# A deeper ring of expert weights, paid for with single buffers, in a mixture-of-experts decoder block

## The chip, the cores and the metric

One core of one Trainium2 chip runs the whole program. The engines are TensorE (PE: matmuls, and PEld: the weight loads that go with them), VectorE (DVE), ScalarE (ACT), GpSimd (POOL) and SyncE (SP). DMAs are issued from the queues of SP, ACT and POOL and carried out by 16 DMA engines that all of them share. The metric is the device time of one execution in microseconds (us), the median of several runs; less is better.

## The reference

The block normalises its input, runs a convolution branch and a differential attention branch, merges the two through gates and an output projection, and then sends each of the 1024 tokens (1024 wide) to 2 of 32 experts. Only the last part is touched by the change:

```python
def expert_block(args):
    toks, wb, e = args
    xb = hf[toks]                                   # 128 gathered rows
    hid = jax.nn.silu(jnp.matmul(xb, w_g[e])) * jnp.matmul(xb, w_u[e])
    return jnp.matmul(hid, w_d[e]) * wb[:, None]
...
y = jnp.zeros_like(hf).at[row_tok].add(yb.reshape(n_rows, D))
```

`w_g` and `w_u` are 1024 x 512 and `w_d` is 512 x 1024 in each of the 32 experts, all float32: 6 MiB of weights for each expert, 192 MiB in all, each used once.

## The kernel before

The program runs through the projections, the attention and the convolution branch, the merge, the output projection with the routing (`out_proj`), and then the experts, one after the other (`experts`).

**Weights.** The weights of an expert arrive in six chunks of 1 MiB (128 partitions x 2048 numbers): two of the gate matrix G, two of the up matrix U, two of the down matrix D. SP issues the loads (`chunk_dma`). A chunk lands in one of the 12 slots of a ring: 11 in the pool mrA, one in mrB, which lies where the merged activations `mg` lay before. The load that takes a slot again waits until the chunk that lay there has been split. From the 18th load on, a load also waits until the load five before it has landed, so at most five are under way.

**Splits.** Matmuls run on pairs of numbers in a shortened float format, a high and a low part, three matmuls for each product (`mm3`, lines 98 to 100). For each chunk ACT writes the high part `ch` (line 93) and DVE the low part `cl` (line 94). Both have four buffers (`nsplit`): the fifth chunk waits until PE is done with the first.

**One expert.** POOL gathers the 128 rows of the expert's tokens from HBM into `gx` (line 1003, an indirect DMA; two buffers, `ngx`). PE transposes them in two halves of four blocks into `pt` (line 1015), ACT and DVE split the result into `xh` and `xl` (two buffers each). PE multiplies by G (24 matmuls) and U (24), ACT and DVE form the hidden tile `sg`, PE transposes it (line 1044), ACT and DVE split it into `dh` and `dl`, PE multiplies by D (24), ACT scales the result into `y` (line 1057, two buffers, `ny`), and POOL adds it to the output in HBM (line 1058, an indirect DMA that adds).

**Order of the work.** Experts overlap: `experts` writes down, for each expert e, the load of expert e+1, a gather, the matmuls by G of e, the transposes of the hidden tile of e-1, the matmuls by U of e, the transposes of the rows of e+1, and the matmuls by D of e-1. A scheduler with its own idea of durations then sets the order on each engine; the order is fixed when the program is built, and each engine works through its list without overtaking. Where the scheduler expects the weights late, it moves the transposes of the next rows forward: in the kernel before, from the rows of expert 23 on, the first of them stand ahead of matmuls by G or U of the expert before, not behind its matmuls by U.

The lines that the change and the prediction speak of: `out_proj` with `mg_split`, which reads `mg` last; `chunk_dma`, `chunk_split`, `gather`, `x_front`, `expert_down` and `experts`; and in `block_kernel` the pools from `mg` to `moe`.

Of the kernel before, what the change touches and what calls it, by code (L numbers as in the profile page):

```python
# [10 lines left out]
F32 = mybir.dt.float32  # L11
F32R = mybir.dt.float32r
# [8 lines left out]
P = 128  # L21
D = 1024
T = 1024
NT = T // P
ND = D // P
# [5 lines left out]
E = 32  # L31
# [18 lines left out]
class Block:  # L50
    def __init__(self, tc, ins, outs, dbg=None):
        self.tc, self.nc = tc, tc.nc
        self.i = ins
        self.out = outs[0]
        self.dbg = dbg or {}
        self.groups = {2: (0, 2), 4: (2, 2), 6: (4, 2), 7: (6, 1)}
        self.modeB, self.modeC = 99, 31
        self.loads, self.window, self.rawA, self.rawB, self.rawC, self.nsplit, self.ny, self.ngx = [], 5, 11, 1, 0, 4, 2, 2

# [947 lines left out]
    def x_front(self, gx):  # L1007
        nc, mp = self.nc, self.xp
        xh = self.xq.tile([P, ND, P], F32R, name="xh", bufs=2)
        xl = mp.tile([P, ND, P], F32R, name="xl", bufs=2)  # L1010
        for k0 in range(0, ND, 4):
            pt = self.ps.tile([P, 4, P], F32, name="pt", tag="T", bufs=2)
            g = gx[:, k0 * P:(k0 + 4) * P].rearrange("t (p k) -> t k p", k=4)
            for k in range(4):
                nc.tensor.transpose(pt[:, k], g[:, k], self.ident)  # L1015
            self.split(xh[:, k0:k0 + 4], xl[:, k0:k0 + 4], pt)
        return xh, xl
# [44 lines left out]
    def chunk_dma(self, src, w):  # L1062
        ring = self.rawA + self.rawB
        q = len(self.loads) % ring
        pool = self.mrA if q < self.rawA else self.mrB
        raw = pool.tile([P, 2048], F32, name="ra")
        d = self.nc.sync.dma_start(raw, src)
        raw = raw.rearrange("p (a b) -> p a b", b=w)
# [7 lines left out]
    def chunk_split(self, raw):  # L1076
        hi = self.xp.tile(list(raw.shape), F32R, name="ch", bufs=self.nsplit)
        lo = self.xp.tile(list(raw.shape), F32R, name="cl", bufs=self.nsplit)
        self.split(hi, lo, raw)
        return [(hi[:, q], lo[:, q]) for q in range(raw.shape[1])]  # L1080
# [9 lines left out]
    def experts(self):  # L1090
        nc, tc = self.nc, self.tc
        mp = self.xp
# [6 lines left out]
        S = [dict() for _ in range(E)]  # L1099
        for k in range(self.ngx - 1):  # L1100
            first = self.gather(col(k), gx[k])
        tok = [mp.tile([P, 1], F32, name=f"tok{k}") for k in range(2)]
# [15 lines left out]
        for e, cur in enumerate(S):  # L1118
            cur["e"] = e
            prev = down(S[e - 1]) if e else iter(())  # L1120
            if e + 1 < E:
                S[e + 1]["raw"] = self.load_raw(e + 1)
            if e + self.ngx - 1 < E:
                self.gather(col(e + self.ngx - 1), gx[(e - 1) % self.ngx])
            if e >= self.modeC:
# [114 lines left out]
def block_kernel(tc, ins, outs, dbg=None):  # L1240
    b = Block(tc, ins, outs, dbg)
# [14 lines left out]
    b.cv = tc.alloc_tile_pool(name="cv", bufs=1, side="right", reuse_waits="tile")  # L1256
    b.mg = [b.mp.tile([P, ND, T // 2], F32, name=f"mg{n}") for n in range(2)]
    with tc.manual_schedule(engines={mybir.EngineType.PE}):
# [30 lines left out]
    b.wo.release()  # L1289
    b.mp.release()  # L1290
    b.xq = tc.alloc_tile_pool(name="moeB", bufs=1, side="right", reuse_waits="tile")
    b.mrB = tc.alloc_tile_pool(name="mrB", bufs=b.rawB, side="right", reuse_waits="tile")
    b.xp = tc.alloc_tile_pool(name="moe", bufs=1, side="right", reuse_waits="tile")
    b.ps = tc.alloc_tile_pool(name="psM", bufs=1, space=PSUM, reuse_waits="tile")
    b.experts()
    b.xp.release()
    b.mrB.release()
    b.xq.release()
    b.mrA.release()
    b.xp = b.xq = tc.alloc_tile_pool(name="ovf", bufs=1, side="right", reuse_waits="tile")  # L1300
# [26 lines left out]
```

## Time and profile before

| | us |
|---|---|
| median of 3 runs | 1393.62 (1393.1 to 1395.93) |
| the profiled execution | 1390.4 |
| its span, first to last instruction | 1388.7 |
| PE busy in the span | 1322.6 (95%) |
| DVE busy | 1059.4 (76%) |
| ACT busy | 787.1 (57%) |
| POOL busy | 169.2 (12%) |

The profiled execution is 3.2 us below the median and 1.7 us above its own span. Busy PE is the time in which some matmul is under way by the profile; where it falls, PE has waited. A stretch of the trace has four columns that matter here: the busy time of PE, the granted clock of PE (PEclk), the share of the DMA engines that is busy, and the rate of all transfers. A row of a timeline gives start, duration, engine, line, operation, output and inputs, and in brackets how long the engine sat idle before it and who ended that.

### The profile page before, as it was taken

What the parts mean: (1) busy time and instruction counts of PE and PEld (TensorE: products, weight loads), DVE (VectorE), ACT (ScalarE), POOL (GpSimd) and SP (SyncE); (2) the same over time, 40 slices, a digit from 0 to 9 for tenths busy, and PEclk for the clock granted to TensorE, in tenths of its full rate; (3) what the DMA queues carried; (4) which work ended last, traced back from release to release, by engine and by line L of the source; (5) the groups of instructions that cost most, each with busy time, mean ns of one, the idle gap of its engine ahead of it and who ended that gap; (6) DMA issues with size and microseconds to landing.
All of it is one profiled execution on the core that took longest, in us unless ns stands there. A gap on an engine that the chain in (4) does not pass through costs nothing.

```text
span 1388.7 us, 18243 instructions
## 1 busy us (share of the span) xinstructions
PE 1322.6 (95%) x6790; PEld 1126.3 (81%) x6790; DVE 1059.4 (76%) x1423; ACT 787.1 (57%) x1109; POOL 169.2 (12%) x324
## 2 busy tenths in 40 slices
PE   6999999999999999999999699999999999999995
PEld 5889999887888888887887578888888888777774
DVE  6776676655788898376367789898888888888893
ACT  5567675653211212442352478888888877777782
POOL 1212121200000000000000111111111121221210
PEclk9999999999999999999999799999999999999998
DMA  6010000102111211024953499999999999999981
GB/s 222 1 46 22 26 21 16 30 24 76 53 53 31 61 45 48 16 65 151 340 197 132 165 337 366 360 364 366 380 378 368 367 367 361 353 364 365 354 319 15
DMA packets 97596, 264.80 MB, mean 191 GB/s; under 512 B 14033, under 2 KB 59234, under 8 KB 72930
## 3 DMA queue, kind: packets, MB, share of 16 engines
q1 hardware_dynamic: 81026, 237.73, 45.6%
q0 software_dynamic: 9216, 16.81, 5.0%
q10 hardware_dynamic: 7264, 9.08, 1.9%
q8 instruction: 54, 0.88, 0.3%
q14 instruction: 36, 0.29, 0.1%
HBM read 255.18 MB, written 25.17 MB: 202 GB/s over the span
## 4 chain that ended last, share of the span: by engine, by line
PE 45%; issue 31%; DMA 9%; DVE 7%; POOL 6%; ACT 2%; POOLq 0%; SPq 0%; DVEq 0%; ACTq 0%
DMA out_dram<-y,idx 7%; PE pg L98 5%; PE pg L99 5%; PE pg L100 5%; POOL out_dram L1058 3%; POOL gx L1003 2%; PE pq L98 2%; PE pq L99 2%; PE pq L100 2%; PE po L362 2%; PE pb L98 2%; PE pb L99 2%; PE pb L100 2%; PE pc L98 2%; PE pc L100 2%
## 5 line engine op out<-in xcount | busy, mean ns | idle before, releaser
L94 DVE TENSOR_TENSOR cl<-ra,ch 128x2048 fp32r<-128x2048 f32 x192 | 435.8, 2288 | 65.3 <-ACT ch L93 62.5
L93 ACT ACTIVATE ch<-ra 128x2048 fp32r<-128x2048 f32 x192 | 364.7, 1919 | 78.1 <-PE pg L100 33.7
L98 PE MATMUL pg<-ch,xh 128*128 128x512 f32 x512 | 203.1, 397 | 4.7 <-ACT ch L93 3.1
L99 PE MATMUL pg<-cl,xh 128*128 128x512 f32 x512 | 202.8, 396 | 2.3 <-DVE cl L94 2.3
L100 PE MATMUL pg<-ch,xl 128*128 128x512 f32 x512 | 201.0, 393 | 0.0
L595 DVE SCALAR_TENSOR_TENSOR ac<-yy,dw,ac 128x1024 f32<-128x1024 f32 x120 | 152.9, 1281 | 2.3
L98 PEld LDWEIGHTS pg<-ch,xh 128*128 128x128 f32 x512 | 96.9, 189 | 26.7 <-ACT ch L93 5.0
L99 PEld LDWEIGHTS pg<-cl,xh 128*128 128x128 f32 x512 | 96.8, 189 | 22.3 <-DVE cl L94 3.1
L100 PEld LDWEIGHTS pg<-ch,xl 128*128 128x128 f32 x512 | 96.6, 189 | 20.1 <-DVE xl L94 0.4
L98 PE MATMUL py<-ch,dh 128*128 128x512 f32 x256 | 102.4, 400 | 1.9 <-ACT dh L93 1.9
L99 PE MATMUL py<-cl,dh 128*128 128x512 f32 x256 | 100.6, 393 | 0.0
L100 PE MATMUL py<-ch,dl 128*128 128x512 f32 x256 | 100.2, 392 | 0.0
L98 PE MATMUL pg<-hTh,whb 128*128 128x512 f32 x256 | 100.2, 391 | 0.0
L99 PE MATMUL pg<-hTl,whb 128*128 128x512 f32 x256 | 99.7, 390 | 0.0
L100 PE MATMUL pg<-hTh,wlb 128*128 128x512 f32 x256 | 99.7, 390 | 0.0
L98 PE MATMUL pq<-wha,hTh 128*128 128x384 f32 x256 | 96.2, 376 | 0.0
L93 ACT ACTIVATE whb<-wrb 128x512 fp32r<-128x512 f32 x48 | 30.0, 632 | 104.1 <-PE pg L99 87.2
L99 PE MATMUL pq<-wla,hTh 128*128 128x384 f32 x256 | 87.4, 341 | 0.7 <-DVE xn1v L65 0.7
L100 PE MATMUL pq<-wha,hTl 128*128 128x384 f32 x256 | 87.4, 341 | 0.0
L1003 POOL DMA_INDIRECT gx<-h2d,idx x32 | 49.3, 1539 | 289.0 <-PE pt L1015 224.4
L1058 POOL DMA_INDIRECT out_dram<-y,idx x32 | 56.4, 1764 | 226.4 <-ACT y L1057 202.8
L331 ACT ACTIVATE ee<-sc,mx 128x128 f32<-128x128 f32 (+7 forms) x64 | 47.2, 746 | 23.1 <-DVE mx L329 23.1
(311 smaller groups left out, 2653.5 us busy)
## 6 DMA issues: line engine op xcount, KB each, us to landing
ra<-in_w_gate_e_dram SPq DMA_DIRECT2D x64, 1024.0 KB
ra<-in_w_up_e_dram SPq DMA_DIRECT2D x64, 1024.0 KB
ra<-in_w_down_e_dram SPq DMA_DIRECT2D x64, 1024.0 KB
wrb<-in_w_in_dram SPq DMA_DIRECT2D x32, 256.0 KB
wra<-in_w_in_dram SPq DMA_DIRECT2D x32, 192.0 KB
wrb<-in_w_in_dram SPq DMA_DIRECT2D x32, 128.0 KB
wro<-in_x_dram SPq DMA_DIRECT2D x16, 256.0 KB
wor<-in_w_out_dram SPq DMA_DIRECT2D x8, 512.0 KB
```

Source lines behind the costliest of these rows:

```text
L93: self.nc.scalar.activation(hi, src, AF.Copy)
L94: self.last_split = (eng or self.nc.vector).tensor_tensor(lo, src, hi.bitcast(F32), op=ALU.subtract).ins
L98: mm(ps, lhsT=lh, rhs=rh, start=first, stop=False)
L99: mm(ps, lhsT=lh, rhs=rl, start=False, stop=False)
L100: mm(ps, lhsT=ll, rhs=rh, start=False, stop=last)
L331: nc.scalar.activation(ee[:, :n], sc[:, :n], AF.Exp, bias=mx, accum_out=s["sm"][qb][:, c:c + 1])
L362: nc.tensor.matmul(po, lhsT=s["at"][j // 4][:, j % 4], rhs=s["V"][j], start=j == 0, stop=j == qb)
L595: nc.vector.scalar_tensor_tensor(ac, yy[:, j:j + T], w(j), ac, op0=ALU.mult, op1=ALU.add)
L1003: return self.nc.gpsimd.indirect_dma_start(out=gx, out_offset=None, in_=self.h2d, in_offset=bass.IndirectOffsetOnAxis(ap=idx, axis=0), bou ...
L1058: nc.gpsimd.indirect_dma_start(out=self.out, out_offset=bass.IndirectOffsetOnAxis(ap=idx, axis=0), in_=y, in_offset=None, bounds_check=T - ...
```

## The change

The ring has 15 slots: 11 in mrA as before, and four that lie in the two tiles of `mg`, two slots in each. `mg` is no longer given back before the experts; instead a pair of slots is one tile with the tag of `mg0` or `mg1`, so the first load into a pair waits until everything that read the tile before is done, the two chunks of the pair before included. The space for this comes from single buffers: one `gx` (the gather of e+1 is issued in iteration e as before), one `xh`, one `xl`, one `y`, and three `cl` in place of four; `ch` keeps four.

```diff
@@ -55,7 +55,7 @@
         self.dbg = dbg or {}
         self.groups = {2: (0, 2), 4: (2, 2), 6: (4, 2), 7: (6, 1)}
         self.modeB, self.modeC = 99, 31
-        self.loads, self.window, self.rawA, self.rawB, self.rawC, self.nsplit, self.ny, self.ngx = [], 5, 11, 1, 0, 4, 2, 2
+        self.loads, self.window, self.rawA, self.nhi, self.nlo, self.ny, self.ngx = [], 5, 11, 4, 3, 1, 1
 
     def rsqrt(self, pool, out, ss, w, mul, tag):
         nc = self.nc
@@ -1006,8 +1006,8 @@
 
     def x_front(self, gx):
         nc, mp = self.nc, self.xp
-        xh = self.xq.tile([P, ND, P], F32R, name="xh", bufs=2)
-        xl = mp.tile([P, ND, P], F32R, name="xl", bufs=2)
+        xh = self.xq.tile([P, ND, P], F32R, name="xh", bufs=1)
+        xl = mp.tile([P, ND, P], F32R, name="xl", bufs=1)
         for k0 in range(0, ND, 4):
             pt = self.ps.tile([P, 4, P], F32, name="pt", tag="T", bufs=2)
             g = gx[:, k0 * P:(k0 + 4) * P].rearrange("t (p k) -> t k p", k=4)
@@ -1060,10 +1060,15 @@
                                      compute_op=ALU.add)
 
     def chunk_dma(self, src, w):
-        ring = self.rawA + self.rawB
+        ring = self.rawA + 4
         q = len(self.loads) % ring
-        pool = self.mrA if q < self.rawA else self.mrB
-        raw = pool.tile([P, 2048], F32, name="ra")
+        if q < self.rawA:
+            raw = self.mrA.tile([P, 2048], F32, name="ra")
+        else:
+            k, half = divmod(q - self.rawA, 2)
+            if half == 0:
+                self.pair = self.mp.tile([P, 2, 2048], F32, name=f"rp{k}", tag=f"mg{k}")
+            raw = self.pair[:, half]
         d = self.nc.sync.dma_start(raw, src)
         raw = raw.rearrange("p (a b) -> p a b", b=w)
         self.loads.append(d.ins)
@@ -1074,8 +1079,8 @@
         return raw
 
     def chunk_split(self, raw):
-        hi = self.xp.tile(list(raw.shape), F32R, name="ch", bufs=self.nsplit)
-        lo = self.xp.tile(list(raw.shape), F32R, name="cl", bufs=self.nsplit)
+        hi = self.xp.tile(list(raw.shape), F32R, name="ch", bufs=self.nhi)
+        lo = self.xp.tile(list(raw.shape), F32R, name="cl", bufs=self.nlo)
         self.split(hi, lo, raw)
         return [(hi[:, q], lo[:, q]) for q in range(raw.shape[1])]
 
@@ -1097,8 +1102,7 @@
             nc.gpsimd.memset(g, 0.0)
         col = lambda e: idx[:, e:e + 1]
         S = [dict() for _ in range(E)]
-        for k in range(self.ngx - 1):
-            first = self.gather(col(k), gx[k])
+        first = self.gather(col(0), gx[0])
         tok = [mp.tile([P, 1], F32, name=f"tok{k}") for k in range(2)]
         with tc.issue_after(first.ins):
             nc.gpsimd.memset(tok[0], 0.0)
@@ -1120,8 +1124,8 @@
             prev = down(S[e - 1]) if e else iter(())
             if e + 1 < E:
                 S[e + 1]["raw"] = self.load_raw(e + 1)
-            if e + self.ngx - 1 < E:
-                self.gather(col(e + self.ngx - 1), gx[(e - 1) % self.ngx])
+            if e + 1 < E:
+                self.gather(col(e + 1), gx[(e + 1) % self.ngx])
             if e >= self.modeC:
                 for _ in prev:
                     pass
@@ -1254,7 +1258,7 @@
     b.mp = tc.alloc_tile_pool(name="mg", bufs=1, side="right", reuse_waits="tile")
     b.wo = tc.alloc_tile_pool(name="wO", bufs=2, side="right", reuse_waits="tile")
     b.cv = tc.alloc_tile_pool(name="cv", bufs=1, side="right", reuse_waits="tile")
-    b.mg = [b.mp.tile([P, ND, T // 2], F32, name=f"mg{n}") for n in range(2)]
+    b.mg = [b.mp.tile([P, ND, T // 2], F32, name=f"mg{n}", tag=f"mg{n}") for n in range(2)]
     with tc.manual_schedule(engines={mybir.EngineType.PE}):
         for _ in range(8):
             next(conv)
@@ -1287,15 +1291,13 @@
     b.ep.release()
     b.we.release()
     b.wo.release()
-    b.mp.release()
     b.xq = tc.alloc_tile_pool(name="moeB", bufs=1, side="right", reuse_waits="tile")
-    b.mrB = tc.alloc_tile_pool(name="mrB", bufs=b.rawB, side="right", reuse_waits="tile")
     b.xp = tc.alloc_tile_pool(name="moe", bufs=1, side="right", reuse_waits="tile")
     b.ps = tc.alloc_tile_pool(name="psM", bufs=1, space=PSUM, reuse_waits="tile")
     b.experts()
     b.xp.release()
-    b.mrB.release()
     b.xq.release()
+    b.mp.release()
     b.mrA.release()
     b.xp = b.xq = tc.alloc_tile_pool(name="ovf", bufs=1, side="right", reuse_waits="tile")
     b.overflow()
```

The scheduler gives the changed kernel other orders at three places that the prediction speaks of.

SP, from the middle of the output projection to the first loads for expert 2 (`wro` are tiles of the block's input for the projection, `ra` the slots of mrA and mrB, `rp` a pair in the space of `mg`). Before:

```order
L789 DMA wro<-in_x_dram 128x512 x2
L751 DMA wor<-in_w_out_dram 128x2x512 x2
L789 DMA wro<-in_x_dram 128x512 x6
L1067 DMA ra<-in_w_down_e_dram 128x2048
L789 DMA wro<-in_x_dram 128x512
L1067 DMA ra<-in_w_gate_e_dram 128x2048 x2
L1067 DMA ra<-in_w_up_e_dram 128x2048 x2
```

And in the changed kernel:

```order
L789 DMA wro<-in_x_dram 128x512 x2
L751 DMA wor<-in_w_out_dram 128x2x512 x2
L789 DMA wro<-in_x_dram 128x512 x2
L1072 DMA rp_7658<-in_w_down_e_dram 128x2048
L789 DMA wro<-in_x_dram 128x512
L1072 DMA rp_7658<-in_w_gate_e_dram 128x2048
L789 DMA wro<-in_x_dram 128x512 x3
L1072 DMA rp_7741<-in_w_gate_e_dram 128x2048
L789 DMA wro<-in_x_dram 128x512
L1072 DMA rp_7741<-in_w_up_e_dram 128x2048
L1072 DMA ra<-in_w_up_e_dram 128x2048
```

The twelfth chunk stands four input tiles earlier, and three more chunks stand ahead of the first load that takes a slot again.

DVE, one expert in the middle of the stage: the split of `dl`, then the low parts of chunks, the hidden tile `sg`, the split of `xl`, and low parts again. Before:

```order
L94 TENSOR_TENSOR dl<-pt,dh 128x512
L94 TENSOR_TENSOR cl<-ra,ch 128x2048
L1031 SCALAR_TENSOR_TENSOR sg<-pg,tbl,sg 128x512
L94 TENSOR_TENSOR cl<-ra,ch 128x2048
L94 TENSOR_TENSOR xl<-pt,xh 128x512 x2
L94 TENSOR_TENSOR cl<-ra,ch 128x2048 x4
```

And in the changed kernel:

```order
L94 TENSOR_TENSOR dl<-pt,dh 128x512
L94 TENSOR_TENSOR cl<-ra,ch 128x2048 x2
L1031 SCALAR_TENSOR_TENSOR sg<-pg,tbl,sg 128x512
L94 TENSOR_TENSOR xl<-pt,xh 128x512 x2
L94 TENSOR_TENSOR cl<-ra,ch 128x2048 x4
```

Between `dl` and `sg` stand now the second chunk of D and the first of the next G; the second chunk of G, which stood ahead of `xl`, stands behind it.

PE, one of the last experts of the changed kernel (expert 28): the rows show where the last transposes of its rows stand, directly ahead of the 24 matmuls by D of expert 26 (`py`):

```order
L98 MATMUL pg<-ch,xh 128x512
L99 MATMUL pg<-cl,xh 128x512
L100 MATMUL pg<-ch,xl 128x512
L1015 MATMUL pt<-ident,gx_7615 128x128 x2
L98 MATMUL py<-ch,dh 128x512
L99 MATMUL py<-cl,dh 128x512
```

and, behind those 24, where the first four transposes of the rows of expert 29 stand:

```order
L99 MATMUL py<-cl,dh 128x512
L100 MATMUL py<-ch,dl 128x512
L98 MATMUL pg<-ch,xh 128x512
L1044 MATMUL pt<-ident,sg 128x128 x4
L1015 MATMUL pt<-ident,gx_7615 128x128 x4
L99 MATMUL pg<-cl,xh 128x512
L100 MATMUL pg<-ch,xl 128x512
```

The kernel before has the transposes of the rows of experts 23 to 31 moved forward in much the same way, but there they read two tiles of rows in turn and here one. In the changed kernel the rows of experts 28, 29, 30 and 31 stand so: 24 matmuls by D, one by G and four transposes of a hidden tile after the last transposes of the rows before. The rows of expert 26 stand 12 matmuls further back, and those of expert 27 follow 23 more matmuls by U. In experts 26 to 30 ACT has `y` ahead of the high part of the second chunk of G; in the middle of the stage, in both kernels, it stands between the two chunks of U.

## Rows read from the trace of the kernel before

**Rows 1.** Stretches of the stage of the experts. Columns: start and end, length, busy time of PE, PEld, DVE, ACT and POOL with their instructions, granted clock, share of the DMA engines, GB/s.

```profile
760.00:780.00 20.00, 12.54 (x114) 11.37 (x114) 17.06 (x103) 5.30 (x13) 0.00 (x0) 0.84 0.14 54
780.00:800.00 20.00, 15.26 (x61) 12.65 (x62) 15.18 (x10) 14.17 (x11) 5.44 (x4) 0.74 0.78 287
...
940.00:1040.00 100.00, 100.00 (x470) 83.77 (x469) 89.19 (x58) 80.83 (x62) 17.11 (x12) 1.00 0.96 377
...
1180.00:1340.00 160.00, 154.60 (x712) 126.72 (x712) 136.03 (x86) 123.30 (x95) 32.20 (x16) 1.00 0.98 361
```

**Rows 2.** POOL's timeline: gathers (L1003) and additions to the output (L1058). The 32 additions stand for experts 0 to 31 in order; shown are those of experts 0, 7, 19, 29 and 31, and the gather behind that of expert 7.

```profile
821.92 1.64 POOL L1058 DMA_INDIRECT out_dram<-y,idx  x1 [5.35 <-ACT y L1057]
...
946.80 1.60 POOL L1058 DMA_INDIRECT out_dram<-y,idx  x1 [5.38 <-ACT y L1057]
958.01 1.26 POOL L1003 DMA_INDIRECT gx<-h2d,idx  x1 [9.61 <-PE pt L1015]
...
1160.88 1.59 POOL L1058 DMA_INDIRECT out_dram<-y,idx  x1 [5.59 <-ACT y L1057]
...
1348.67 1.55 POOL L1058 DMA_INDIRECT out_dram<-y,idx  x1 [16.03 <-ACT y L1057]
...
1375.33 1.55 POOL L1058 DMA_INDIRECT out_dram<-y,idx  x1 [16.07 <-ACTq L1180]
```

**Rows 3.** SP's waits from 760 to 850 us: who waited, for whom, us in total, times, longest.

```profile
SPq L1067 <- DVE cl L94: 70.0, 15, 29.6
```

**Rows 4.** The same from 1150 to 1250 us.

```profile
SPq L1067 <- DMA ra<-in_w_down_e_dram: 32.7, 10, 4.5
...
SPq L1067 <- DVE cl L94: 0.3, 1, 0.3
```

**Rows 5.** All instructions on the chunks: duration min/median/max in ns, first and last start.

```profile
L94 DVE TENSOR_TENSOR cl<-ra,ch x192: 2277/2291/2300, 781.8 to 1362.7; 128x2048 fp32r<-128x2048 f32 x192
...
L1067 SPq DMA_DIRECT2D ra<-in_w_down_e_dram x64: 327/328/545, 664.6 to 1344.4; - x64
```

**Rows 6.** DVE's last reads of the two tiles of `mg`, in the output projection (the rows with `ml`; the first is that of the last quarter of `mg0`, the second that of the last quarter of `mg1`).

```profile
721.13 1.22 DVE L94 TENSOR_TENSOR ml<-mg,mh 128x1024 fp32r<-128x1024 f32 x1
...
752.52 1.22 DVE L94 TENSOR_TENSOR ml<-mg,mh 128x1024 fp32r<-128x1024 f32 x1
```

**Rows 7.** SP's issues in the same stretch: the twelfth chunk, and the first load that takes a slot again.

```profile
746.04 0.43 SPq L1067 DMA_DIRECT2D ra<-in_w_down_e_dram  x1
...
784.08 0.33 SPq L1067 DMA_DIRECT2D ra<-in_w_gate_e_dram  x1
```

**Rows 8.** PE in one expert of the middle of the stage: the eight transposes of rows, the first of the 24 matmuls by D, the first by G, the four transposes of the hidden tile, the first by U.

```profile
956.61 1.12 PE L1015 MATMUL pt<-ident,gx 128*128 128x128 f32 x8
957.49 0.47 PE L98 MATMUL py<-ch,dh 128*128 128x512 f32 x1
...
963.04 0.39 PE L98 MATMUL pg<-ch,xh 128*128 128x512 f32 x1
...
968.49 0.63 PE L1044 MATMUL pt<-ident,sg 128*128 128x128 f32 x4
968.88 0.48 PE L98 MATMUL pg<-ch,xh 128*128 128x512 f32 x1
```

**Rows 9.** The gathers from 770 to 790 us: from issue to landing.

```profile
DMA to landing us min/median/max: 4.3/7.7/8.4
```

**Rows 10.** The gathers from 950 to 1050 us: from issue to landing.

```profile
DMA to landing us min/median/max: 8.6/8.7/10.1
```

**Rows 11.** The gathers from 1250 to 1300 us: from issue to landing.

```profile
DMA to landing us min/median/max: 9.4/9.5/10.5
```

**Rows 12.** ACT in the same expert of the middle: the high part of the first chunk of U, `y`, and the two chunks behind it.

```profile
960.52 1.92 ACT L93 ACTIVATE ch<-ra 128x2048 fp32r<-128x2048 f32 x1 [0.82 <-PE py L100]
963.24 1.12 ACT L1057 ACTIVATE y<-py,tbl 128x1024 f32<-128x1024 f32 x1 [0.80 <-PE py L100]
964.25 3.72 ACT L93 ACTIVATE ch<-ra 128x2048 fp32r<-128x2048 f32 x2
```

**Rows 13.** DVE in the same expert: `sg`, the two splits of `xl`, and the low part of a chunk.

```profile
958.26 0.75 DVE L1031 SCALAR_TENSOR_TENSOR sg<-pg,tbl,sg 128x512 f32<-128x512 f32 x1
...
961.12 1.28 DVE L94 TENSOR_TENSOR xl<-pt,xh 128x512 fp32r<-128x512 f32 x2
962.48 2.29 DVE L94 TENSOR_TENSOR cl<-ra,ch 128x2048 fp32r<-128x2048 f32 x1
```

**Rows 14.** ACT at the end: `y` of experts 29 and 30.

```profile
1347.28 1.12 ACT L1057 ACTIVATE y<-py,tbl 128x1024 f32<-128x1024 f32 x1 [1.21 <-PE py L100]
...
1354.99 1.12 ACT L1057 ACTIVATE y<-py,tbl 128x1024 f32<-128x1024 f32 x1 [0.79 <-PE py L100]
```

**Rows 15.** DVE at the end: the low part of the last chunk and the last hidden tile.

```profile
1362.74 2.29 DVE L94 TENSOR_TENSOR cl<-ra,ch 128x2048 fp32r<-128x2048 f32 x1 [0.29 <-ACT ch L93]
1365.65 0.75 DVE L1031 SCALAR_TENSOR_TENSOR sg<-pg,tbl,sg 128x512 f32<-128x512 f32 x1 [0.62 <-PE pg L100]
```

**Rows 16.** The additions to the output from 950 to 1050 us: from issue to landing.

```profile
DMA to landing us min/median/max: 10.1/10.4/10.6
```

**Rows 17.** The chain that ended last: start, duration, what. One piece near the end.

```profile
1348.67 8.29 DMA out_dram<-y,idx
```

**Rows 18.** PE before the first expert: the first transposes of rows and what they waited for.

```profile
784.74 1.95 PE L1015 MATMUL pt<-ident,gx 128*128 128x128 f32 x8 [5.56 <-DMA gx<-h2d,idx]
```

## The prediction

> **What bounds the kernel now.** I read the stretches of the stage of the experts first [rows 1], then POOL's timeline as a clock of the experts [rows 2], then SP's waits [rows 3, 4] and one expert on PE, ACT and DVE [rows 8, 12, 13].
>
> The stretches show PE without a gap from 940 to 1040 us and, from 1180 to 1340 us, 154.60 of 160 us busy, with the DMA engines at 0.96 and 0.98: something starves PE late that did not early. POOL's clock gives the sizes. From expert 0 (821.92) to expert 19 (1160.88) an expert takes 338.96 / 19 = 17.84 us, to the hundredth the same each time: PE's own pace. From expert 19 to 29 (1348.67) it takes 187.79 / 10 = 18.78 us. That is the pace of the weights: the first load into a used slot goes out at 784.08 [rows 7], the last of the 180 such loads at 1344.4 [rows 5], so 560.3 / 180 = 3.11 us each and 18.7 us for the six of an expert. So the loads fall behind PE by about 0.85 us for each expert; the 12 chunks that lie ready at 784 us hide that until expert 20, and then PE waits. SP's waits agree: early it waits for slots (70.0 us on `cl` in 90 us), late almost only for its own loads (0.3 us on `cl` in 100 us). The starved stretch costs 187.79 - 178.4 = 9.4 us against PE's own pace.
>
> **The change, part by part.**
>
> *The ring.* DVE reads `mg0` for the last time until 722.35 and `mg1` until 753.74 [rows 6]. So the twelfth chunk can go at 722 in place of 746 us [rows 7], and three more at about 754, 30 us before the first slot is free again; from 754 to 784 the DMA engines have little to do (0.14 busy from 760 to 780 [rows 1]). The tile of the input that SP issues between them is wanted only by the last projection, so I put that at nothing (at most 0.4 us). Three chunks more are 3 x 3.11 = 9.3 us of lead, 11 experts at 0.85 us, and the starved stretch begins with expert 20: all of it goes, -9.4 us. A pair is loaded again only when both its chunks are split; that makes the ring 14 deep at worst and costs nothing while loads, not slots, are late; if the lead were lost altogether, 0 and not -9.4.
>
> *Three low buffers.* A low part waits now for the chunk three before it. I lay the new order of DVE into the expert of [rows 8]: U of this expert ends at 956.6 us, the halves of D end at 960.3 and 963.0, of the next G at 965.8 and 968.5. With 2.29 us for a low part [rows 5], 0.75 for `sg` and 1.28 for `xl` [rows 13], G's first chunk is ready at 958.9, `xl` at 960.8, G's second at 963.1, U's at 965.3 and 968.0, D's first (which waits for the end of G) at 970.7, its second at 974.0. PE wants them at 963.0, 965.8, 968.9, 971.6, 975.3 and 978.1, `xl` at 963.3: at least 2.5 us later each time. So nothing for experts 0 to 24; if one of them were late by 0.5 us, 24 times, +12.
>
> *One `xh`, one `xl`.* PE's last read of the old ones is at 956.6 us, before the new transposes; the splits come after those in any case. Nothing. *One `y`, middle.* The addition issued at 946.80 lands 10.4 us later [rows 2, 16], at 957.2, and ACT writes the next `y` at 963.24 [rows 12]. Nothing.
>
> *One `gx`.* A gather can only go when the transposes of the rows before are done, and the next transposes wait for it. In the middle the eight transposes end at 957.73, POOL issues at 958.01 [rows 2, 8], the rows land 8.7 us later [rows 10] at 966.7, and PE wants them one expert later, at 974.4. Nothing, for experts 0 to 25. But for experts 28, 29, 30 and 31 the order of PE puts the transposes of the next rows behind 24 matmuls by D (957.49 to 963.04, 5.55 us), one by G (0.23) and four transposes (0.39) [rows 8]: 6.2 us after the start of D. The gather lands 0.52 + 8.7 = 9.2 us after that start. PE waits 3.0 us. Late in the kernel gathers took 9.5 us [rows 11], which gives 3.8; with the longest of those rows, 10.5, 4.8. I take a landing of 9.0, nearer to the early rows, since the new order issues the gather at the place where the early ones go: 3.35 us, four times, +13.4 (12.0 to 19.2). For expert 26 the cover is 5.55 + 0.23 + 0.39 + 12 x 0.227 = 8.9 us: +0.6 (0 to 2.1). For expert 27 it is over 11 us: nothing.
>
> The Trainium skill (DMA: Bandwidth & Descriptors, Anatomy of one DMA) gives for a DMA from GpSimd about 2.0 us plus its bytes at 436 GB/s. By that rule the rows of an expert, at most 0.52 MB, would land in 3.2 us, an estimate from that page, inside the cover of 6.2, and the sum would lose its 13.4 and 0.6 us. The trace disagrees: its shortest gather, with no load under way, takes 4.3 us [rows 9], and those that run beside the loads 8.6 and more [rows 10, 11].
>
> *ACT's new place for `y`.* In experts 26 to 30 the high part of the second chunk of G stands behind `y`, which waits for D. From the end of D: `y` starts after 0.20 us, the chunk 1.01 later (963.04, 963.24, 964.25 [rows 8, 12]), then 1.92 for the high and 2.29 for the low part: 5.4 us. PE is there after 0.23 + 0.39 + 0.4 + 12 x 0.227 = 3.7 us. In expert 26 that is a wait of 1.7 us (0 to 2); in the four behind it the wait for the gather covers it.
>
> *One `y`, end.* Of experts 29 and 30, `y` stand 7.71 us apart (1347.28, 1354.99 [rows 14]), but the addition of the first is issued at 1348.67 and takes 8.29 us [rows 17]; ACT would write the second at 1357.0, 2.0 us later. Behind it on ACT stand the high parts of the last three chunks; the last low part has 0.62 us to spare before `sg` [rows 15]. +1.4 (0 to 2.4). The start, where the clearing of the one `gx` waits for more than before, I put at 0 (within 1).
>
> The sum: -9.4 + 13.4 + 0.6 + 1.7 + 1.4 = +7.7 us on the profiled execution (1390.4), that is 1398.1. The median of the runs lies 3.2 above that execution, so I set the sum on it: 1393.6 + 7.7 = 1401.3 us.
>
> **The rivals.**
>
> *A: the rows come in time, and only the ring counts: faster.* For it: that gathers are otherwise never waited for, and the skill's rule; against it: every gather beside the loads took 8.6 us or more, and the order of PE leaves 6.2. It needs a landing under 5.6 us. -9.4 + 1.7 + 1.4 = -6.3: 1387.3 us.
>
> *B: the lead is not gained.* Pairs and the in-order queue of SP give the chunks away again, the loads starve PE from expert 20 on as before, and the waits for the gathers come on top from 28 on. For it: SP waited 70 us for slots early; against it: the three chunks need only an idle stretch. Six experts at 0.94 us more than the forecast, +5.6: 1406.9 us.
>
> *C: the waits lower PE's clock.* After PE had stood for 5.56 us before its first expert [rows 18], the granted clock was 0.84 and 0.74 in two stretches of 20 us [rows 1]: 8.4 us of a full clock. Against it: waits of 3 to 4 us between full stretches are shorter than that one. Once: 1401.3 + 8.4 = 1409.7 us.
>
> *D: the two halves cancel.* Gathers at 8.6 us, no wait in expert 26 and none at the end: -9.4 + 11.8 = +2.4: 1396.0 us, no change that can be told.
>
> **How the numbers follow.** The forecast has a chance of 0.60, A 0.10, B 0.13, C 0.08, D 0.09. A measurement of this kernel tells a difference from about 0.2%, 2.8 us. Faster is A, 0.10; same is D, 0.09; slower is the rest, 0.81. The forecast's own range goes from 1396 (all terms at their low ends) to 1409 (landings at 10.5); it covers D and B, and with a microsecond below for the start that is 1395 to 1409.
>
> **What would show it.** In the profile of the changed kernel, POOL's additions should stand 17.84 us apart up to expert 23, and about 21 us apart for experts 26 to 29. PE should have four waits of 3 to 4 us on `pt` of line 1015, released by the DMA of `gx`, all behind 1270 us, and hardly any on loads. If PE starves on loads before expert 25, the ring was overrated; if additions are further apart than 17.84 in the middle, the low buffers were; if the four waits are missing, the term of the gathers is wrong and the kernel is faster.

## The result and the profile after

| | before | after |
|---|---|---|
| median of the runs compared, us | 1393.36 | 1407.86 (1405.6 to 1412.0, 4 runs) |
| ratio to before | | 1.0105, 95% interval [1.0082, 1.0128] |
| the profiled execution | 1390.4 | 1405.6 |
| its span | 1388.7 | 1403.9 |
| mean granted clock of PE | 0.989 | 0.985 |

The kernel became slower by 14.5 us. The forecast was 1401.3 us, 7.7 us slower, with a range from 1395 to 1409. The times of the four runs follow their mean granted clock (1405.6 us at 0.985, 1406.07 at 0.984, 1409.64 at 0.981, 1412.0 at 0.980); the profiled execution is the fastest of them, so what it shows for the clock is the least of the four.

First the clock of the experts, POOL's additions after the change: that of expert 0, and those of experts 23 to 31 in order.

```profile
820.66 2.23 POOL L1058 DMA_INDIRECT out_dram<-y,idx  x1 [4.84 <-ACT y L1057]
...
1230.97 2.19 POOL L1058 DMA_INDIRECT out_dram<-y,idx  x1 [3.96 <-ACT y L1057]
1250.45 1.59 POOL L1058 DMA_INDIRECT out_dram<-y,idx  x1 [10.82 <-ACT y L1057]
1270.10 1.59 POOL L1058 DMA_INDIRECT out_dram<-y,idx  x1 [4.93 <-ACT y L1057]
1293.35 1.59 POOL L1058 DMA_INDIRECT out_dram<-y,idx  x1 [4.90 <-ACT y L1057]
1316.35 1.59 POOL L1058 DMA_INDIRECT out_dram<-y,idx  x1 [4.89 <-ACT y L1057]
1337.85 1.59 POOL L1058 DMA_INDIRECT out_dram<-y,idx  x1 [4.66 <-ACT y L1057]
1362.00 2.11 POOL L1058 DMA_INDIRECT out_dram<-y,idx  x1 [22.56 <-ACT y L1057]
1370.12 2.10 POOL L1058 DMA_INDIRECT out_dram<-y,idx  x1 [6.02 <-ACT y L1057]
1390.62 1.55 POOL L1058 DMA_INDIRECT out_dram<-y,idx  x1 [18.39 <-ACTq L1184]
```

From 820.66 to 1230.97 the experts 0 to 23 stand (1230.97 - 820.66) / 23 = 17.84 us apart, where before the pace was lost at expert 19 [rows 2]. Then 19.48, 19.65, 23.25, 23.00, 21.50 and 24.15 us. From expert 0 to 29 it takes 541.34 us, 23.98 over PE's pace (29 x 17.84 = 517.36); before, it was 1348.67 - 821.92 = 526.75, 9.4 over it. That is +14.6 of the 15.2 us between the two profiled executions. Expert 0 is 1.26 us earlier, the two experts at the end take 28.62 in place of 26.66 us, and what follows the last addition is 0.1 us shorter.

What PE waited for from 1180 us on (who, for whom: us in total, times, longest):

```profile
PE pt L1015 <- DMA gx<-h2d,idx: 16.4, 5, 4.8
PE py L98 <- ACT dh L93: 1.7, 2, 1.0
PE pg L99 <- DVE cl L94: 1.4, 1, 1.4
PE pt L1044 <- DVE sg L1031: 0.8, 1, 0.8
```

In the kernel before, PE waited from 1180 us on for the parts of late chunks:

```profile
PE pg L98 <- ACT ch L93: 3.1, 4, 1.4
PE pg L99 <- DVE cl L94: 2.3, 3, 1.1
```

After the change no line names `ch`, and ACT, which takes the chunks first, waits 2.2 us for loads from 1150 to 1362 us where it waited 14.9 before: the starving on weights is gone. Five waits for the rows stand in its place. They are, in PE's timeline, with that for the low part of G's second chunk (`cl`) among them, and with some of the matmuls that follow the first long wait:

```profile
1234.36 0.72 PE L1015 MATMUL pt<-ident,gx 128*128 128x128 f32 x4 [1.35 <-DMA gx<-h2d,idx]
...
1254.35 0.50 PE L99 MATMUL pg<-cl,xh 128*128 128x512 f32 x1 [1.39 <-DVE cl L94]
...
1272.98 1.10 PE L1015 MATMUL pt<-ident,gx 128*128 128x128 f32 x4 [3.61 <-DMA gx<-h2d,idx]
...
1275.16 0.63 PE L99 MATMUL pg<-cl,xh 128*128 128x512 f32 x1
1275.59 0.63 PE L100 MATMUL pg<-ch,xl 128*128 128x512 f32 x1
...
1277.37 0.39 PE L100 MATMUL pg<-ch,xl 128*128 128x512 f32 x1
1277.60 0.39 PE L98 MATMUL pg<-ch,xh 128*128 128x512 f32 x1
...
1295.89 0.72 PE L1015 MATMUL pt<-ident,gx 128*128 128x128 f32 x4 [3.26 <-DMA gx<-h2d,idx]
...
1319.00 0.72 PE L1015 MATMUL pt<-ident,gx 128*128 128x128 f32 x4 [3.38 <-DMA gx<-h2d,idx]
...
1341.93 1.10 PE L1015 MATMUL pt<-ident,gx 128*128 128x128 f32 x4 [4.80 <-DMA gx<-h2d,idx]
```

The first wait (1.35) is that for the rows of expert 26, the last four (3.61, 3.26, 3.38, 4.80; 15.05 us) are those for experts 28 to 31. The gathers from 1180 us on landed like this, the line that answers to [rows 11]; the profile has a landing for only two of the eight. Behind it stand POOL's gathers of the rows of experts 28 and 31:

```profile
DMA to landing us min/median/max: 9.2/9.5/9.9
...
1263.45 1.71 POOL L1003 DMA_INDIRECT gx<-h2d,idx  x1 [11.42 <-PE pt L1015]
...
1331.21 1.98 POOL L1003 DMA_INDIRECT gx<-h2d,idx  x1 [13.28 <-PE pt L1015]
```

From the start of the gather to the transposes that waited for it, it is 9.5 us for expert 28 and 10.7 for expert 31; for experts 26, 29 and 30 (gathers at 1224.34, 1286.71 and 1309.70) it is 10.0, 9.2 and 9.3 us.

Behind the wait at 1272.98 the matmuls take 0.63 us and start 0.43 us apart; from about 1276.4 on they take 0.39 again and start 0.23 apart. The stretches (columns as in [rows 1]) show it as the granted clock:

```profile
1180.00:1340.00 160.00, 144.15 (x660) 119.30 (x658) 122.42 (x79) 110.28 (x88) 28.01 (x16) 0.98 0.99 363
...
1250.00:1260.00 10.00, 8.61 (x39) 6.78 (x39) 7.54 (x5) 8.85 (x8) 1.59 (x1) 1.00 0.99 364
...
1270.00:1280.00 10.00, 7.02 (x26) 5.87 (x27) 7.38 (x4) 5.70 (x4) 1.59 (x1) 0.83 1.00 349
...
1290.00:1300.00 10.00, 6.74 (x28) 5.45 (x27) 6.69 (x4) 7.00 (x5) 1.59 (x1) 0.85 1.00 364
...
1320.00:1330.00 10.00, 10.00 (x46) 8.26 (x45) 7.41 (x6) 6.26 (x5) 0.00 (x0) 1.00 1.00 354
...
1340.00:1350.00 10.00, 8.07 (x33) 6.83 (x34) 6.79 (x4) 4.07 (x4) 0.00 (x0) 0.83 0.28 93
...
1380.00:1390.00 10.00, 8.31 (x28) 6.08 (x28) 1.74 (x5) 1.37 (x2) 0.00 (x0) 0.83 0.00 1
```

From 1180 to 1340 us PE is busy 144.15 of 160 us (before 154.60 [rows 1]) while the DMA engines are as full as before (0.99). In three stretches of 10 us with a long wait the clock is 0.83 or 0.85: PE spent a part of each at the lower of its two levels, 1.2 GHz, which costs at most 1.7 + 1.5 + 0.2 (the stretch from 1300 had 0.98) + 1.7 = 5.1 us of a full clock. So the late experts' 23.98 us are 16.4 for rows, 1.4 for G's second chunk and 5.1 of clock, 22.9 together; 1.1 us is not assigned.

### The profile page after: what moved, and what is told of

It is laid out like the page before. It is cut to its first block, busy times and chain, and to the rows that moved or that the text cites. A ratio compares the mean times of both kernels' runs of the same rounds, so it can differ in the third digit from the quotient of the medians.

```text
span 1403.9 us, 18382 instructions
## 1 busy us (share of the span) xinstructions
PE 1325.2 (94%) x6790; PEld 1129.1 (80%) x6790; DVE 1059.5 (75%) x1423; ACT 786.5 (56%) x1109; POOL 187.3 (13%) x323
## 4 chain that ended last, share of the span: by engine, by line
PE 44%; DMA 23%; issue 23%; DVE 6%; ACT 2%; POOL 2%; POOLq 0%; SPq 0%; DVEq 0%; ACTq 0%
DMA gx<-h2d,idx 15%; DMA out_dram<-y,idx 6%; PE pg L98 4%; PE pg L100 4%; PE pg L99 4%; PE pq L98 2%; PE pq L99 2%; PE pq L100 2%; PE po L362 2%; PE pb L98 2%; PE pb L99 2%; PE pb L100 2%; PE pc L98 2%; PE pc L100 2%; PE pc L99 2%
## 5 line engine op out<-in xcount | busy, mean ns | idle before, releaser
L94 DVE TENSOR_TENSOR cl<-ra,ch 128x2048 fp32r<-128x2048 f32 x143 | 326.3, 2289 | 57.1 <-ACT ch L93 41.9
L93 ACT ACTIVATE ch<-ra 128x2048 fp32r<-128x2048 f32 x143 | 271.4, 1919 | 44.8 <-PE pg L100 22.2
L94 DVE TENSOR_TENSOR cl<-rp,ch 128x2048 fp32r<-128x2048 f32 x49 | 111.7, 2287 | 16.2 <-ACT ch L93 10.9
L100 PEld LDWEIGHTS pg<-ch,xl 128*128 128x128 f32 x512 | 97.3, 190 | 20.6 <-DVE xl L94 0.4
L93 ACT ACTIVATE ch<-rp 128x2048 fp32r<-128x2048 f32 x49 | 93.5, 1915 | 17.9 <-ACT ch L93 6.9
L1003 POOL DMA_INDIRECT gx<-h2d,idx x32 | 59.2, 1851 | 307.1 <-PE pt L1015 234.3
L1058 POOL DMA_INDIRECT out_dram<-y,idx x32 | 65.4, 2043 | 190.2 <-ACT y L1057 171.8
```

What stands on the lines that cost most here:

```text
L93: self.nc.scalar.activation(hi, src, AF.Copy)
L94: self.last_split = (eng or self.nc.vector).tensor_tensor(lo, src, hi.bitcast(F32), op=ALU.subtract).ins
L100: mm(ps, lhsT=ll, rhs=rh, start=False, stop=last)
L1003: return self.nc.gpsimd.indirect_dma_start(out=gx, out_offset=None, in_=self.h2d, in_offset=bass.IndirectOffsetOnAxis(ap=idx, axis=0), bou ...
L1058: nc.gpsimd.indirect_dma_start(out=self.out, out_offset=bass.IndirectOffsetOnAxis(ap=idx, axis=0), in_=y, in_offset=None, bounds_check=T - ...
```

## The experiments

The theory after this result: a single row tile makes the gather wait for the transposes of the expert before, and PE's order puts too little work between; the price is set by that order and by the clock. The rivals: the waits would have cost the same as loads (nothing is lost by the tile); the ring itself gives its lead away; the single `y` or the three low parts cost. The tuple in the diffs is (window, chunks in `mrA`, high parts, low parts, `y`, `gx`); chunks in the ring are `mrA`'s and four.

**Two row tiles in the changed kernel.** PE's order stays the same.

```diff
-        ... self.nhi, self.nlo, self.ny, self.ngx = [], 5, 11, 4, 3, 1, 1
+        ... self.nhi, self.nlo, self.ny, self.ngx = [], 5, 11, 4, 3, 1, 2
```

> The changed kernel with two tiles for gathered rows again, all else as changed; the order of PE is the same, instruction by instruction. Theory (the single tile of rows costs the time, by the waits for the gather in the last experts and the clock behind them): the distances of 23.25, 23.00, 21.50 and 24.15 us between the last additions go back to about 17.84, the four waits on the transposes go, and the kernel takes 1407.9 - 20.5 - 1.6 = about 1386 us, faster than the kernel before. Rival (the low buffers, the single result or the loads are what is late there): the distances stay above 21 us and the time above 1400.

1389.8 us, ratio to before 0.9981 [0.9967, 0.9994]. Against the changed kernel that is 18 us. What is left of PE's waits from 1180 us on, and the stretch:

```profile
PE pg L99 <- DVE cl L94: 4.1, 3, 1.4
PE pg L98 <- ACT ch L93: 2.7, 2, 1.3
```

```profile
1180.00:1340.00 160.00, 153.22 (x717) 126.66 (x716) 132.34 (x84) 119.68 (x94) 27.14 (x16) 1.00 0.98 360
```

The waits for rows are gone and with them the lowered clock (1.00). Five waits of 1.3 to 1.4 us remain, one in each of five late experts, which the profile puts down to `cl` three times and to `ch` twice. In each of them ACT has written `y` just before it splits G's second chunk, as in expert 26 of the changed kernel, and experts 25 to 29 stand 19.5 to 19.6 us apart. These 6.8 us are why this run does not come down to the theory's 1386. The kernel keeps all 15 chunks and still has room for the second tile: the space that the single row tile saved was not needed for the ring.

**The changed kernel in the written order.** PE then has all eight transposes of the next rows behind U, and a whole expert lies between two experts' transposes.

```diff
-    b.experts()
+    with tc.manual_schedule(engines={mybir.EngineType.PE}):
+        b.experts()
```

> The changed kernel, all its single buffers kept, with PE held to the order in which the experts are written, so that the transposes of the next rows stand behind all matmuls by U in every expert. Theory (it is the single tile of rows together with the transposes moved forward): the gather has a whole expert of time again, all additions stand 17.84 us apart to the end, no wait on the transposes; about 1384 us. Rival (single buffers of x, result or low parts cost time of their own): over 1393 us.

1390.79 us, ratio 0.999 [0.9978, 1.0001]: the same as before. PE waits for no row though there is one tile: the tile costs nothing where the order gives the gather time. But the loads are late again; ACT from 1240 to 1350 us:

```profile
ACT ch L93 <- DMA ra<-in_w_up_e_dram: 5.7, 5, 1.8
ACT ch L93 <- DMA ra<-in_w_gate_e_dram: 4.4, 6, 1.4
```

The additions stand 17.84 to 17.94 us apart to expert 25 and 18.26 to 19.30 from there to expert 29; from expert 0 to 29 it takes 521.29 us, 3.9 over PE's pace where before had 9.4. The two kernels have different orders; what the ring is worth in one and the same order is told below, by the kernel before and by a ring of 12 chunks.

**One row tile in the kernel before.** Gathers go one expert ahead in place of two.

```diff
-        self.loads, ... self.nsplit, self.ny, self.ngx = [], 5, 11, 1, 0, 4, 2, 2
+        self.loads, ... self.nsplit, self.ny, self.ngx = [], 5, 11, 1, 0, 4, 2, 1
...
-        for k in range(self.ngx - 1):
-            first = self.gather(col(k), gx[k])
+        first = self.gather(col(0), gx[0])
...
-            if e + self.ngx - 1 < E:
-                self.gather(col(e + self.ngx - 1), gx[(e - 1) % self.ngx])
+            if e + 1 < E:
+                self.gather(col(e + 1), gx[(e + 1) % self.ngx])
```

> The kernel before with one tile of gathered rows and nothing else. Theory: its late order of PE leaves the gather 6.2 us in every second expert from 25 on (rows of experts 25, 27, 29 and 31), so four waits of 3 to 4 us with a drop of the clock behind them, of which the loads, late there anyway, take back up to 9.4 us: 1400 to 1408 us. Rival (a single tile of rows is hidden): 1393 us as before.

1425.17 us, ratio 1.023 [1.0203, 1.0257]: 32 us slower, far over both expectations. PE's waits from 820 us on, and the stretch:

```profile
PE pt L1015 <- DMA gx<-h2d,idx: 20.6, 5, 5.9
PE pg L98 <- ACT ch L93: 6.3, 4, 1.6
```

```profile
1180.00:1340.00 160.00, 140.66 (x615) 115.56 (x616) 112.79 (x72) 101.09 (x79) 24.55 (x15) 0.94 0.81 309
```

From expert 0 to 29 it takes 558.23 us, 40.9 over PE's pace, where before had 9.4. Of the 40.9, 20.6 are waits for rows, 6.3 waits for `ch`, and up to 13.7 the lowered clock (stretches of 10 us from 1160 to 1390 us, 0.66 at the lowest; a part of it falls into the waits themselves). The waits for `ch` are not the loads': ACT waits for loads 0.7 us from 1140 us on, and the DMA engines are 0.81 busy, no longer the bound. So the loads did give back their 9.4, as expected. What both expectations lacked is a fifth wait, the longest (5.9 us, the rows of expert 23, which have only 13 matmuls by D and four transposes before them), a loss by the clock as large as three or four waits, and the waits for `ch`.

**The kernel before in the written order** (the same edit as above).

> The kernel before (ring of 12, double buffers) with PE held to the written order. Theory (the kernel before is paced by its loads from expert 20 on, not by the order): 1393 us, unchanged within 0.3%, the additions 18.7 to 18.8 us apart late. Rival (the order moved by the scheduler was itself the loss of the kernel before, and the ring gives nothing): about 1384 us, 17.84 us apart to the end.

1394.89 us, ratio 1.001 [0.9995, 1.0024]: the same. The order alone gains nothing where loads pace the end. By the additions this kernel is 7.0 us over PE's pace to expert 29 (524.39 us), and the one with 15 chunks in the same order 3.9; by the times they are 4.1 us apart, at the edge of what the intervals can tell.

**The ring back to 12 chunks, in the written order.**

```diff
-        ... self.ngx = [], 5, 11, 4, 3, 1, 1
+        ... self.ngx = [], 5, 8, 4, 3, 1, 1
```

> The changed kernel with PE held to the written order and the ring back to 12 chunks; single row tile, three low parts, single `y` stay. Theory (the three more chunks are worth 5 to 6 us there, since with 15 the loads were late from expert 25 or 26 on and with 12 they are from 20 on): 1395 to 1397.5 us; PE starved from expert 20 to 22 on, additions 18.7 apart. Rival (the ring gives its lead away in this order, and what that run has over the kernel before comes from the order): 1390 to 1392.5.

1395.99 us, ratio 1.0025 [1.0012, 1.0039]: with 15 chunks it was 1390.79. The three chunks are worth 5.2 us by the times and 6.7 by the additions (528.02 us, 10.7 over PE's pace, in place of 3.9). ACT waits for loads already from 1150 to 1240 us, where with 15 chunks it had no such wait:

```profile
ACT ch L93 <- DMA ra<-in_w_gate_e_dram: 8.9, 10, 1.4
ACT ch L93 <- DMA rp<-in_w_up_e_dram: 3.8, 2, 2.2
```

**The ring back to 12, 13 and 14 chunks in the changed kernel**, with the scheduler's order (8, 9 and 10 in the place of 11).

> The changed kernel with the ring back to 12 chunks; single row tile, three low parts, single `y` and the engines' orders stay. Theory (the ring is worth what the loads would cost before the waits for the rows begin; from expert 26 on these waits give the loads 3 to 5 us an expert, so that PE no longer starves): the experts 20 to 25 take 18.7 in place of 17.84 us, 5 us, and the time is 1411 to 1414. Rival 1 (the prediction's full term): 1416 to 1419. Rival 2 (the waits for the rows hide the loads altogether, the ring buys nothing): 1407 to 1409.

1436.46 us, ratio 1.0309 [1.0288, 1.033]: 28.6 us above the changed kernel, where none of the three expectations had more than 11. PE's order tells why. With 12 chunks the scheduler moves the transposes of the next rows forward from expert 19 on, and the rows of eight experts have 24 matmuls by D, one by G and four transposes (6.1 us) between them and the rows before; with 15 it begins at expert 26 and there are four. From this came the expectations for the two other sizes:

> The changed kernel with a ring of 13 chunks. Its PE order puts 24 matmuls by D, one by G and four transposes (6.1 us) between the rows of ten experts and those before (18 to 20, 23 to 27, 30, 31), against four in the changed kernel and eight with 12 chunks; three more have 8.6 to 8.8 us. Theory (the time goes by the number of experts so ordered: 3.76 us of waiting each as in the changed kernel, 1.35 for one with 8.8, and about 1.3 of a lowered clock for each long wait): 10 x 3.76 + 3 x 1.35 = 41.7 us of waits against 16.4, 1440 us, between 1433 and 1448, slower than with 12 chunks (1436.5). Rival (the chunks themselves count: more of them, less starving): between the times with 12 and 15 chunks, 1420 to 1432.

> The changed kernel with a ring of 14 chunks. Five experts (26 to 30) have 6.1 us between their rows and those before, two (24, 25) 8.6 to 8.8. Theory (as for 13 chunks): 5 x 3.76 + 2 x 1.35 = 21.5 us of waits against 16.4, and a lowered clock once more: 1414, between 1411 and 1419. Rival (the chunks count, evenly between 12 and 15): a third of 28.6 above the changed kernel, 1417.4; if the pair makes 15 chunks no better than 14, 1408.

PE's waits from 820 us on with 12, then 13, then 14 chunks:

```profile
PE pt L1015 <- DMA gx<-h2d,idx: 29.6, 8, 4.4
PE pt L1015 <- DVE dl L94: 5.3, 1, 5.3
```

```profile
PE pt L1015 <- DMA gx<-h2d,idx: 38.3, 12, 4.4
PE pt L1015 <- DVE cl L94: 4.6, 1, 4.6
```

```profile
PE pt L1015 <- DMA gx<-h2d,idx: 19.0, 7, 4.3
```

The waits of 5.3 and 4.6 us that the profile puts down to `dl` and `cl` also stand at transposes of rows with the cover of 6.1 us. With 13 chunks POOL starts the gather at 1106.44, it lands 10.4 us later, at 1116.84, and PE goes on at 1117.01: that wait is for the rows. With 12 chunks the profile has no landing for the gather in question; the wait (5.3 us) is counted with the rows here, which is not shown.

| chunks | experts with 6.1 us | with 8.6 to 8.8 us | waits for rows, us | for G's second chunk | lowered clock, at most | expert 0 to 29, over PE's pace | time, us | ratio to before |
|---|---|---|---|---|---|---|---|---|
| 15 (the change) | 4 | 1 | 16.4 | 1.4 | 5.1 | 24.0 | 1407.86 | 1.0105 [1.0082, 1.0128] |
| 14 | 5 | 2 | 19.0 | 1.9 | 13.6 | 34.1 | 1414.45 | 1.0145 [1.0116, 1.0174] |
| 12 | 8 | 2 | 34.9 | 4.2 | 15.3 | 56.4 | 1436.46 | 1.0309 [1.0288, 1.033] |
| 13 | 10 | 3 | 42.9 | 2.8 | 20.4 | 67.1 | 1449.31 | 1.0408 [1.038, 1.0436] |

The clock's column is summed over stretches of 10 us of the one profiled execution. In each kernel the waits for rows, those for G's second chunk and the clock together come within some 2 us of the distance over PE's pace. 13 chunks are slower than 12: the number of experts with the short cover goes with the time, not the number of chunks. The same 12 chunks in the written order took 1395.99 us, 40 us less. Loads are not the bound with 12 and 13 chunks (the DMA engines are 0.78 and 0.77 busy from 1180 to 1340 us). 14 came out on the figure forecast (1414), with less waiting than expected (19.0 for 21.5) and more lost to the clock, so the hit is partly luck; 13 was 9 us above its figure (1440), a microsecond over its range.

**Two `y` in the changed kernel** (the orders of all engines stay).

```diff
-        ... self.ngx = [], 5, 11, 4, 3, 1, 1
+        ... self.ngx = [], 5, 11, 4, 3, 2, 1
```

> The changed kernel with two `y` and nothing else undone; the order on the engines stays as it is. Theory (the prediction's term for one `y` at the end, 1.4 us, measured at about 2 us): 1405.5 to 1407, and experts 29 to 31 take 26.7 us in place of 28.6; the four waits for the rows stay. Rival 1 (the single `y` also costs in the middle or in the late experts, where ACT writes it ahead of G's second chunk): below 1404. Rival 2 (it costs nothing): 1407.5 to 1408.5.

1408.38 us, ratio 1.0105 [1.0079, 1.013]: the single `y` costs nothing that can be told. Its profile seems at first to speak against that, as experts 29 to 31 take 26.98 us in place of 28.62. But ACT in the changed kernel did not wait for the addition; its `y` of expert 30 was released by PE:

```profile
1368.73 1.12 ACT L1057 ACTIVATE y<-py,tbl 128x1024 f32<-128x1024 f32 x1 [0.80 <-PE py L100]
```

The addition of expert 29, issued at 1362.00, had landed by then, in under 6.8 us: no load was under way any more (DMA share 0.14 from 1340 to 1360 us). And the kernel with one `y` and two row tiles took 27.04 us there. What made the end 1.6 us longer after the change is the granted clock of 0.83 from 1380 to 1390 us (1.7 us); with two `y` it is 1.00 from 1380 to 1395 us. This run also tells how far the clock differs between executions: with the same orders and nearly the same waits for rows (17.7 us in place of 16.4) its granted clock from 1180 to 1340 us is 0.96 in place of 0.98, and from expert 0 to 29 it is 28.5 us over PE's pace in place of 24.0.

**Versions that might beat both.** Two `y` and the written order:

> The changed kernel with PE held to the written order (as in the run with one y) and with two `y`. Theory (in the written order the tail alone still pays for the single `y`: in the run with one, ACT's last `y` waited about 4 us for the addition before it, and the additions of experts 29 and 31 lie 30.3 us apart against 26.7 in the kernel before): that wait goes, experts 29 to 31 take 26.5 to 28 us, and the time is 1386 to 1388.5 us, below both kernels. Rival (the last chunks, not `y`, are what the end waits for): 1390 to 1392, as with one `y`.

1389.25 us, ratio 0.9977 [0.9963, 0.9991], between the two expectations and not told apart from the run with one `y` (1390.79). The profiled end took 30.5 us, with one `y` 30.3. But the clock is 0.83 in two stretches of 10 us there (from 1350 and from 1370 us) and in one with one `y`, so what sets the end in this order, the loads that still come until 1350 us or the clock, is not shown. Two row tiles, two `y` and 14 chunks in that order:

> Written order on PE, two `y`, two row tiles, ring of 14 chunks in place of 15. Theory (in the written order the single row tile costs nothing, since a row's transposes stand a whole U and more behind the gather): nothing is gained by the second tile, and one chunk less costs up to 3 us: 1387 to 1391, at or above the run with 15 chunks, one row tile and two `y`. Rival (the single row tile still costs, through the place of the gather in the queues): 1 us or more below that run.

1390.05 us, ratio 0.9972 [0.9959, 0.9986]: the same. A second tile in place of one chunk gains nothing there, as the theory had it; the two were not taken apart. And, with two `y` and 15 chunks, the written order only up to expert 30:

> Two `y`, ring of 15, one row tile, PE held to the written order up to expert 30 and left to the scheduler behind it. Theory (with the rows out of the way the end of the kernel waits for the loads, whose pace no order changes): within 1.5 us of the run with two `y` in the written order throughout (1389.25), so 1388 to 1391. Rival (the written order's end is what costs, experts 29 to 31 took 30 us there against 27 in the scheduled order): 1385 to 1387.

1388.36 us, ratio 0.9955 [0.994, 0.9969]. It is the fastest of all, 5 us or 0.45% below the kernel before, but its interval overlaps that of the two others: that the last experts' order is what gained is not shown.

## Why the prediction was right, and where not

The sign and the mechanism of the rows were right; the size was half of it. By its own steps, on the profiled execution:

| step | predicted, us | found, us |
|---|---|---|
| the ring: starved stretch | -9.4 | -9.4 (no wait on loads left) |
| rows of experts 28 to 31 | +13.4 | +15.05 |
| rows of expert 26 | +0.6 | +1.35 |
| expert 26, G's second chunk | +1.7 | +1.4 |
| lowered clock in the late experts | 0 (rival C) | +5.1 |
| late experts, not assigned | | +1.1 |
| the end | +1.4, by `y` | +1.96, of it 1.7 by the clock |
| start | 0 | -1.26 |
| behind the last addition | | -0.1 |
| sum | +7.7 | +15.2 |

*The step that failed most is the one that left the clock out.* The prediction had it as rival C, "against it: waits of 3 to 4 us between full stretches are shorter than that one", with a chance of 0.08. Three of the four long waits did lower it, and a fourth stretch at the end has it too: 6.8 us in all. That this is near C's 8.4 is chance: C took its figure from two stretches around the start of the first expert, where the clock had fallen before the wait of 5.56 us (779.18 to 784.74) began (the granted clock from 775 to 779 us is 0.50). The time, 1407.86, lies between the forecast and C (1409.7), nearer to C. It lies in the forecast's range, but the upper end of that range was set for later landings, and what filled it was mostly the clock: that too is partly luck. The Trainium skill (TensorE: Matmul & The Clock Gate, What's actually happening) has the clock fall to half after PE has been idle. The matmuls behind the wait at 1272.98, 0.43 us apart in place of 0.23, agree with that; the drop at the end, behind waits of 0.85 and 0.69 us, is not explained by it.

*The gathers' landing.* The place, the four experts and the cover were right. I took 9.0 us "nearer to the early rows"; to the transposes it was 9.2 to 10.7, and a wait was 3.76 us on average against 3.35. The late rows [rows 11], which gave 3.8, were the better source. The rule of the Trainium skill that was weighed there (DMA: Bandwidth & Descriptors, Anatomy of one DMA), 3.2 us by an estimate and no wait, does not hold for these gathers. All five waits speak against it.

*The ring.* PE starved no more, as forecast, but not for the reason given alone. Three chunks outlast the late experts only because PE itself was held up there: in the written order, where nothing holds it, the loads were late again from expert 26 on, and the ring was worth 4 to 5 us by the times (1394.89 and 1395.99 with 12 chunks, 1390.79 with 15). The step divided the lead of 9.3 us by a loss of 0.85 us for each expert and got 11 experts; with 15 chunks in the written order the pace was lost at expert 25, six later than in the kernel before (19) and eight later than with 12 chunks in that order (17). What took the rest of it, the pairs or SP's queue (rival B's reasons), was not tried.

*The parts put at nothing.* Three low parts, one `xh`, one `xl` and one `y` in the middle: the 17.84 us to expert 23 bear it out. Apart from `y` they were not undone one by one.

*The end.* One `y` was put at 1.4 us from the 8.29 us of [rows 17]; without loads beside it the addition is faster, and the term is nothing.

*Rival A* (only the ring counts, 1387.3) is what the kernel with two row tiles should have been; it took 1389.8, since the wait for G's second chunk falls in five late experts (6.8 us) once the rows no longer cover it; the step had it once (1.7 us).

## What to carry to other kernels

Before a buffer that a transfer fills is made single, look up in the order what stands between the last read of the old contents and the first of the new, for each place where the scheduler changes that order, and set it against the landing beside the other transfers: here 6.1 us against 9.2 to 10.7. A change of one pool's size can move the place where a scheduler begins to reorder, so count the places anew in each build: 13 chunks were slower than 12. And waits on PE as long as these (3.3 to 4.8 us) are to be priced with the clock behind them: here up to 5.1 us on 16.4 in the profile of the change, and up to 13.6 on 19.0 in that with 14 chunks.

## What was unexpected in the hardware

PE's granted clock fell after waits of 3.61, 3.26 and 4.80 us in a stage that was otherwise full, and not after those of 1.35, 1.39 and 3.38 us; with two `y` it fell with waits of 3.74, 4.39 and 4.85 us and not after one of 3.27. At the lower level a matmul took 0.63 in place of 0.39 us. It also fell at the end of the changed kernel, behind waits of only 0.85 and 0.69 us:

```profile
1380.14 0.74 PE L1044 MATMUL pt<-ident,sg 128*128 128x128 f32 x4 [0.85 <-DVE sg L1031]
1381.57 0.50 PE L98 MATMUL py<-ch,dh 128*128 128x512 f32 x1 [0.69 <-ACT dh L93]
```

The kernel before has the same two waits, from 1365 to 1368 us, at a full clock (1.00 from 1360 to 1370 us); why the one and not the other stays open. Where the long waits were more, the clock from 1180 to 1340 us was lower: 0.98 with three of them in the changed kernel, and 0.94, 0.93 and 0.91 with five of them with 12, 13 and 14 chunks. An addition to the output that took 10.4 us beside the loads [rows 16] landed in under 6.8 us without them.
